# A hybrid attention block on one core: longer distances between dependent steps in chunks two to four, the norm's table a quarter ahead, the last output weights behind the branches'

## The chip, the core and the metric

The kernel runs on 1 core of one Trainium2 chip. The metric is device time in microseconds (us) of one execution; the time of a kernel is the median of its runs. TensorE (PE in the profile, PEld its weight loads) multiplies, VectorE (DVE), ScalarE (ACT) and GpSimd (POOL) do the rest, and SyncE (SP) issues nearly all transfers, in one queue.

## What is computed

One layer over 2048 tokens of width 1024, in float32, with two mixers side by side:

```python
def hybrid_layer(x, w_in, conv_w, a_log, dt_bias, dn_norm_w, sinks, w_branch, w_out, ln_g, ln_b, cos, sin):
    h = jnp.einsum("bsd,dc->bsc", x, w_in)
    ...
    o_a = chunked_gated_delta_rule(q_a, k_a, v_a, g, beta)
    ...
    y_b = banded_sink_attention(q_b, k_b, v_b, sinks) * jax.nn.silu(sw_z)
    merged = (jax.nn.sigmoid(gate_a) * jnp.einsum("bsc,cd->bsd", y_a, w_branch[0])
              + jax.nn.sigmoid(gate_b) * jnp.einsum("bsc,cd->bsd", y_b, w_branch[1]))
    out = jnp.einsum("bsd,de->bse", merged, w_out)
    r = (DEEPNORM_ALPHA * x + out).astype(jnp.float32)
    ...
    y = (r - mu) * lax.rsqrt(var + LN_EPS) * ln_g.astype(jnp.float32) + ln_b.astype(jnp.float32)
```

Branch A is a gated delta rule with 4 heads of 128: inside a block a triangular inverse, from block to block a state S per head that each block reads and updates. Branch B is attention over a window of 128 tokens with 8 query heads of 64 and a learned sink in each softmax.

## The kernel before

**Tiling.** The sequence is cut into four chunks of 512 tokens (T), each of four blocks of 128 (NB). Every large product is done as three matmuls on a high and a low part (`prods`, L184 to L186), so that a piece of dense work is a run of 128x512 or 128x256 matmuls. The split weights are kept in DRAM after chunk one (`kw_...`) and loaded again in each later chunk, 512 KB a load, through four buffers `wb` (L160).

**The order of the work** on TensorE is the order in which the program issues it; a small planner, the class `Order`, works it out while the program is written. It has a clock `now` in nanoseconds. Dense pieces (`dense`) advance it by their cost: PE_R = 216 for a 512-column matmul. Between the bits of a dense piece, `run` issues every small task that has come due. A small task is a generator that yields (cost, distance): its next step is due that distance after this one, which is the time the other engines are given to get its operands ready. If a dense piece needs a task to be over, `finish(name)` jumps the clock from due time to due time and issues the steps without dense work between them:

```python
    def finish(self, name):
        while name not in self.done:
            self.run()
            if name not in self.done:
                self.now = min(t[0] for t in self.tasks)
```

The order of the dense pieces of a chunk stands in two strings, ORDER_FIRST for chunk one and ORDER for the others: `g` a gate, `kv`, `k0`, `q0`, `v0`, ... projections of branch A's heads and of the window, `w0` and `w1` the window's queries (`window_q`), `z` SiLU paths, `p` the output projection of the chunk before. A chunk's `kv`, `k0` and `q0` are issued early, between the branch pieces of the chunk before. VectorE, ScalarE and the queues get their order from the framework's scheduler, which goes by the order of the program and by what it takes to be ready.

**The small tasks.** The distances are the constants `LAT_...` in L40.
- `decays` (L299 on): the decay factors, with a step of 2000 between its sums and its transposes (L322).
- `front` of a head: transposes and products of q and k (L382, L395, L406, L426, L432), LAT_B apart. After L406 the blocks go to DRAM and back (L417, L419) to be inverted on VectorE (`inverse`, L947, L948); the result goes to DRAM (L445).
- `levels`: fetches the inverse (L458), waits LAT_D, and builds it up in four steps (L470, L477, L486, L491), LAT_B apart.
- `back`: the chain through the state. For each of four blocks L517 (reads S), L522 (reads `bt` of L519) and L528 (reads `wc` of L524, then L529 updates S), LAT_S apart: 12 steps a head.
- `query_rows`: transposes of the rotated queries (L584), LAT_Q after their projection. `window_q` itself calls `finish("qT0")` right behind the projection.
- `attend`: for each block of the window the scores (L610, L611), the softmax on VectorE and ScalarE (L618 to L630), LAT_SM later the transposes (L637), then the values (L645).
- `layer_norm` of the chunk before, on VectorE alone: four steps of statistics, then for each quarter of the width a table of 256 KB (L725, from `in_lnp`) and four steps with it (L727, L728).

`head_in` of head 3 calls `finish("back1")` ahead of k, and of head 2 `finish("vdone1")` ahead of v.

**The end.** In chunk four `branch_b` and `branch_a` (eight pieces each) load their weights `kw_b` as they go. Ahead of branch A's second and fifth piece `last_weights` loads a half of the first output weights (`kw_o`, 8 loads of 256 KB each time, L158) into buffers that x no longer needs; `last_project` uses them.

Of the kernel before, what the change touches and what calls it, by code (L numbers as in the profile page):

```python
# [8 lines left out]
F32 = mybir.dt.float32  # L9
# [30 lines left out]
LAT_INV, LAT_B, LAT_S, LAT_N, LAT_SM, LAT_D, LAT_M, LAT_K, LAT_Q, LAT_Y, LAT_F, LAT_W = 29600, 2700, 2300, 7700, 9200, 11000, 9000, 1400, 7900, 11500, 4100, 2300  # L40
# [4 lines left out]
ORDER = "kv k0 q0 v0 k1 p p p p q1 g w0 v1 z0 k2 q2 v2 g g g k3 z1 g q3 g w1 v3 g g g g z2 g g g z3 g g g"  # L45
# [18 lines left out]
def build(tc, xt, xn, wk, wg, par, lnp, cst, out, seq=2048):  # L64
    nc = tc.nc
    NCH = seq // T
    with ExitStack() as ctx:
# [196 lines left out]

        def window_kv(c):

            ww, more = [], ([w.rearrange("p (k c) -> p k c", k=2) for w in split(("kv", i), wk[i // 2, :, 528 * (i % 2):528 * (i % 2) + 528], 528)]
                            for i in range(4))
            ba = sm.tile([P, NB, 8], F32, name="ba")
            c.vs = [c.prev.vs[4] if c.i else None]  # L270
            for b0 in (0, 2):
                pss = [mm.tile([P, T], F32, name="mm")[:, :264] for _ in range(2)]
                yield from prod_tc(pss, (b0, b0 + 1), c.xh, c.xl, ww if b0 else kept(more, ww), lambda k: load_x(c, k))
                for b, ps in zip((b0, b0 + 1), pss):
                    if b >= 2:
# [8 lines left out]
            st.spawn("decay", decays(c, ba), LAT_Y)  # L284
# [14 lines left out]
        def decays(c, ba):  # L299
# [19 lines left out]
            yield 2 * 426, 2000  # L319
# [49 lines left out]
        def front(c, h):  # L369
# [22 lines left out]
            yield 4 * PE_T, LAT_B  # L392
# [10 lines left out]
            yield PE_R, LAT_B  # L403
# [7 lines left out]
            yield 4 * PE_F, LAT_B  # L411
# [17 lines left out]
            yield 4 * PE_T, LAT_B  # L429
# [6 lines left out]
            st.spawn(f"levels{h}", levels(c, h, m2, q_), max(LAT_B, t0 + LAT_INV - st.now))  # L436
            st.spawn(f"back{h}", back(c, h, k4, q_, ktl, qd, dt, cc, ksum, qsum), max(LAT_B, t0 + LAT_INV - st.now))
            yield 4 * PE_F, 0

        def inverse(h, su, xi):  # L440

            with tc.issue_after(next(i for i in reversed(nc.cur_bb.bb.instructions) if i.engine == mybir.EngineType.DVE)):
                nc.vector.memset(view(su, 33, [[66, 16]]), 0.0)
            yield from small_inverse(tc, pt.tile([P, 256], F32, name="xt"), su, xi.rearrange("p (c i) -> p c i", i=32))
            nc.sync.dma_start(out=at(scr_p[h % 2], 0, [[P, P], [1, P]]), in_=xi)  # L445
            yield None, 0

        def levels(c, h, m2, q_):
# [11 lines left out]
            yield 0, LAT_D  # L460
# [12 lines left out]
            yield 8 * PE_Q, LAT_B  # L473
# [9 lines left out]
            yield 12 * PE_Q, LAT_B  # L483
# [4 lines left out]
            yield 4 * PE_T, LAT_B  # L488
# [4 lines left out]
            yield 4 * PE_T, LAT_B  # L493

        def back(c, h, k4, q_, ktl, qd, dt, cc, ksum, qsum):
# [17 lines left out]
            yield 4 * PE_T, LAT_B  # L513
            psO = p4()
            for b in range(NB):
# [4 lines left out]
                yield PE_F, LAT_S  # L520
# [5 lines left out]
                yield 2 * PE_F, LAT_S  # L526
# [4 lines left out]
                yield 2 * PE_F, LAT_S  # L531
# [29 lines left out]
        def window_q(c, gp):  # L561

            if gp:
                st.finish("window0")
            c.qT = [pa.tile([P, NB, 2, P], F32R, name=n, bufs=1) for n in ("qT0", "qT1")]
            pss = [mm.tile([P, 2, 256], F32, name="mm") for _ in range(2)]
            yield from prod_all(pss, c.xh, c.xl, quarters([f"q{gp}{i}" for i in range(2)]), lambda k: load_x(c, k))
            for b0 in (0, 2):
                if b0:
                    st.finish("qT0")  # L570
                qr = [pa.tile([P, 256], F32, name="kr") for _ in range(2)]
                for b in range(2):
                    rope(nc, sm, qr[b], pss[b0 // 2][:, b], 4, cos[:, c.i * NB + b0 + b], sin[:, c.i * NB + b0 + b])
                st.spawn(f"qT{b0}", query_rows(c, b0, qr), LAT_Q)
# [19 lines left out]
        def attend(c, gp):  # L594
# [8 lines left out]
            for b in range(NB):  # L603
# [27 lines left out]
                yield 8 * PE_T, LAT_SM  # L631
# [80 lines left out]
        def layer_norm(c):  # L712
            fs = []
            for b in range(NB):
# [6 lines left out]
                yield None, 2500  # L721
            for eg in range(4):
                es = slice(256 * eg, 256 * eg + 256)
                lg = pa.tile([P, 2, 256], F32, name="s")
                nc.sync.dma_start(out=lg, in_=bass.AP(tensor=lnp.tensor, offset=lnp.offset + 256 * eg, ap=[[0, P], [D, 2], [1, 256]]))  # L725
                for r, rs, mu in fs:
                    nc.vector.scalar_tensor_tensor(r[:, es], r[:, es], mu, lg[:, 0], ALU.subtract, ALU.mult)  # L727
                    nc.vector.scalar_tensor_tensor(r[:, es], r[:, es], rs, lg[:, 1], ALU.mult, ALU.add)  # L728
                    yield None, 1800
# [70 lines left out]
        for i in range(NCH):  # L800
# [24 lines left out]
            for d in range(KT):  # L825
                if i == NCH - 1 and d in (1, 4):
                    last_weights(c, d // 3)
                st.dense([branch_a(c, d)])
# [195 lines left out]
```

## Time and profile before

| | us |
|---|---|
| median of 3 runs (lowest, highest) | 1668.41 (1666.62, 1669.23) |
| the profiled execution | 1672.24 |
| its span, first to last instruction | 1670.4 |
| TensorE busy in it | 1618.9 |
| VectorE, ScalarE, GpSimd busy | 969.3, 596.2, 92.9 |

Mean granted TensorE clock in the profiled execution: 0.986 of full. The end of a matmul in the profile is modelled, since matmuls are pipelined: from start to start is what one costs, and idle time is counted from the modelled end of the one before. A row of waits names the engine, the tile that it writes and the line, then what came last among the things it waited for: us in total, times, longest. Chunk one ends at about 412 us, two at 830, three at 1240; chunk four's gates end at 1570, and the last projection begins at about 1615.

### The profile page before, as it was taken

To read this page: it belongs to the slowest core of one execution; us is meant where nothing else is said; L and a number is where in the kernel's file an instruction comes from. 1 tells how busy PE (TensorE), PEld (TensorE's weight loads), DVE (VectorE), ACT (ScalarE), POOL (GpSimd) and SP (SyncE) were. 2 spreads that over 40 slices of the span, in tenths; PEclk is the share of its full clock that TensorE was granted. 3 is DMA by queue.
4 is the path that set the end of the run, shared out by engine and by line. 5 is a ranking of instruction groups with operands and counts; after the bars stand their busy time and mean duration, and the time that the engine had idled before them with its cause. 6 is when DMAs were issued, how large, how long until landed. Compare 5 with 4: busy or idle time off the path is not lost.

```text
span 1670.4 us, 26939 instructions
## 1 busy us (share of the span) xinstructions
PE 1618.9 (97%) x9846; PEld 1368.2 (82%) x9846; DVE 969.3 (58%) x3005; ACT 596.2 (36%) x1688; POOL 92.9 (6%) x142
## 2 busy tenths in 40 slices
PE   8999999999998999999999999999999999999998
PEld 6877878787987878788898878888889887878788
DVE  5777687459566656323747774623482866462145
ACT  3565455424213533441301452433230254233110
POOL 2100000000000001000000000000000100000000
PEclk9999999999999999999999999999999999999999
DMA  8876575776867446457666644646666654555862
GB/s 310 260 232 222 184 245 190 244 235 216 273 207 213 135 130 168 142 163 237 191 213 205 199 128 145 172 137 190 202 190 210 221 162 119 166 162 145 284 214 83
DMA packets 189157, 323.37 MB, mean 194 GB/s; under 512 B 31072, under 2 KB 45408, under 8 KB 188896
## 3 DMA queue, kind: packets, MB, share of 16 engines
q1 hardware_dynamic: 185184, 316.40, 60.6%
q0 software_dynamic: 3840, 5.25, 1.5%
q8 instruction: 78, 1.28, 0.3%
q14 instruction: 55, 0.45, 0.1%
HBM read 244.97 MB, written 71.37 MB: 189 GB/s over the span
## 4 chain that ended last, share of the span: by engine, by line
PE 82%; DVE 7%; DMA 7%; ACT 2%; issue 1%; SPq 1%; POOL 0%; DVEq 0%; ACTq 0%; POOLq 0%
PE mm L184 22%; PE mm L186 22%; PE mm L185 22%; PE pp L645 2%; PE pp L637 2%; DMA s<-in_lnp 2%; DMA w<-in_xt 1%; PE pp L610 1%; PE pp L611 1%; PE pd L432 1%; DVE wb L165 1%; PE pd L517 1%; PE pd L528 1%; DMA xl<-kw_o 1%; PE pd L406 1%
## 5 line engine op out<-in xcount | busy, mean ns | idle before, releaser
L184 PE MATMUL mm<-xh,wb 128*128 128x512 f32 x1128 | 468.6, 415 | 0.0
L186 PE MATMUL mm<-xh,wb 128*128 128x512 f32 x1128 | 448.0, 397 | 0.0
L185 PE MATMUL mm<-xl,wb 128*128 128x512 f32 x1128 | 446.8, 396 | 0.0
L186 PEld LDWEIGHTS mm<-xh,wb 128*128 128x128 f32 x1128 | 213.7, 189 | 50.3
L184 PEld LDWEIGHTS mm<-xh,wb 128*128 128x128 f32 x1128 | 214.5, 190 | 45.6 <-issue 6.5
L185 PEld LDWEIGHTS mm<-xl,wb 128*128 128x128 f32 x1128 | 215.2, 191 | 38.8
L184 PE MATMUL mm<-wb,xh 128*128 128x256 f32 (+1 forms) x384 | 113.5, 296 | 1.8 <-DVE kr L899 0.9
L184 PE MATMUL mm<-wb,s 128*128 128x256 f32 x384 | 110.4, 287 | 0.0
L185 PE MATMUL mm<-wb,xh 128*128 128x256 f32 (+1 forms) x384 | 108.9, 284 | 0.0
L186 PE MATMUL mm<-wb,xl 128*128 128x256 f32 (+1 forms) x384 | 108.7, 283 | 0.0
L185 PE MATMUL mm<-wb,s 128*128 128x256 f32 x384 | 108.4, 282 | 0.0
L186 PE MATMUL mm<-wb,s 128*128 128x256 f32 x384 | 108.4, 282 | 0.0
L165 DVE TENSOR_TENSOR wb<-w,wb 128x512 fp32r<-128x512 f32 (+1 forms) x110 | 75.4, 686 | 46.3 <-ACT wb L164 45.5
L164 ACT ACTIVATE wb<-w 128x512 fp32r<-128x512 f32 (+1 forms) x110 | 69.1, 629 | 84.4 <-PE mm L186 58.1
L623 ACT ACTIVATE s<-s,nm 128x256 f32<-128x256 f32 (+1 forms) x128 | 62.5, 490 | 57.1 <-DVE nm L620 56.6
L947 DVE TENSOR_TENSOR xt<-su,xi 128x16 f32<-128x16 f32 (+15 forms) x256 | 76.3, 298 | 5.3
L948 DVE TENSOR_REDUCE xi<-xt 128x8 f32<-128x16 f32 (+15 forms) x256 | 74.6, 291 | 4.9
L184 PEld LDWEIGHTS mm<-wb,xh 128*128 128x128 f32 x384 | 72.9, 190 | 2.7 <-issue 2.5
L184 PEld LDWEIGHTS mm<-wb,s 128*128 128x128 f32 x384 | 73.1, 190 | 0.8
L185 PEld LDWEIGHTS mm<-wb,xh 128*128 128x128 f32 x384 | 72.9, 190 | 0.5
L185 PEld LDWEIGHTS mm<-wb,s 128*128 128x128 f32 x384 | 73.0, 190 | 0.1
L186 PEld LDWEIGHTS mm<-wb,s 128*128 128x128 f32 x384 | 73.0, 190 | 0.0
(660 smaller groups left out, 2997.4 us busy)
## 6 DMA issues: line engine op xcount, KB each, us to landing
wb<-kw_h SPq DMA_DIRECT2D x96, 512.0 KB, 4.1
wb<-kw_g SPq DMA_DIRECT2D x96, 512.0 KB, 4.0
w<-in_wg SPq DMA_DIRECT2D x106, 256.0 KB, 4.2
wb<-kw_b SPq DMA_DIRECT2D x48, 512.0 KB, 4.4
wb<-kw_o SPq DMA_DIRECT2D x36, 512.0 KB, 4.1
kw_h<-wb SPq DMA_DIRECT2D x32, 512.0 KB, 3.9
kw_g<-wb SPq DMA_DIRECT2D x32, 512.0 KB, 3.7
wb<-kw_q SPq DMA_DIRECT2D x24, 512.0 KB, 3.9
```

The source lines that it names most:

```text
L164: nc.scalar.activation(hi, raw, AF.Copy)
L165: nc.vector.tensor_tensor(lo, raw, hi.bitcast(F32), ALU.subtract)
L184: nc.tensor.matmul(ps, sh, mh, start=(first and i == 0), stop=False, skip_group_check=shared)
L185: nc.tensor.matmul(ps, sh, ml, start=False, stop=False, skip_group_check=shared)
L186: nc.tensor.matmul(ps, sl, mh, start=False, stop=(last and i == n), skip_group_check=shared)
L406: nc.tensor.matmul(psKK[:, b], k4[:, b], k4[:, b], start=True, stop=True)
L432: nc.tensor.matmul(psKQ[:, b], k4[:, b], q4[:, b], start=True, stop=True)
L623: nc.scalar.activation(ss[v][:, g, k0:], ss[v][:, g, k0:], AF.Exp, bias=nm[:, v, g:g + 1], scale=0.125, accum_out=su[:, v, g:g + 1])
L637: nc.tensor.transpose(psp[:, kb, g], ss[v][:, g, P * kb:P * kb + P], ident)
L645: nc.tensor.matmul(psY[64 * v:64 * v + 64], c.vs[b + kb][:, 64 * v:64 * v + 64], pTs[v][:, kb], start=(kb == kbs[0]), stop=(kb == 1))
L947: nc.vector.tensor_tensor(tx[:, :, :, :n], u, x, ALU.mult)
L948: nc.vector.tensor_reduce(xi[:, :, i:i + 2], tx[:, :, :, :n], AX.X, ALU.add)
```

## The change

The distances become pairs, the first for chunk one and the second for the others; chunk one's are as before. One gate moves from ahead of `w1` to behind it. The norm's steps are spaced wider, and its table for a quarter is fetched one quarter ahead. `last_weights` is issued with an edge to the latest SP instruction, so that its loads come behind it in the queue.

```diff
-LAT_INV, LAT_B, LAT_S, LAT_N, LAT_SM, LAT_D, LAT_M, LAT_K, LAT_Q, LAT_Y, LAT_F, LAT_W = 29600, 2700, 2300, 7700, 9200, 11000, 9000, 1400, 7900, 11500, 4100, 2300
+LAT_INV, LAT_N, LAT_M, LAT_K, LAT_F, LAT_W = 29600, 7700, 9000, 1400, 4100, 2300
+
+LAT_B, LAT_S, LAT_SM, LAT_D, LAT_Q, LAT_Y, LAT_G = (2700, 3300), (2300, 2900), (9200, 11500), (11000, 13000), (7900, 10500), (11500, 11500), (2000, 3500)
...
-ORDER = "kv k0 q0 v0 k1 p p p p q1 g w0 v1 z0 k2 q2 v2 g g g k3 z1 g q3 g w1 v3 g g g g z2 g g g z3 g g g"
+ORDER = "kv k0 q0 v0 k1 p p p p q1 g w0 v1 z0 k2 q2 v2 g g g k3 z1 g q3 w1 g v3 g g g g z2 g g g z3 g g g"
...
+        latest = lambda engine: next(i for i in reversed(nc.cur_bb.bb.instructions) if i.engine == engine)
...
-            yield 2 * 426, 2000
+            yield 2 * 426, LAT_G[c.i > 0]
...
-            yield 4 * PE_T, LAT_B
+            yield 4 * PE_T, LAT_B[c.i > 0]
...
         def layer_norm(c):
-            fs = []
+            fs, lgs = [], []
+
+            def load_lg(eg):
+                lgs.append(pa.tile([P, 2, 256], F32, name="s"))
+                nc.sync.dma_start(out=lgs[eg], in_=bass.AP(tensor=lnp.tensor, offset=lnp.offset + 256 * eg, ap=[[0, P], [D, 2], [1, 256]]))
+
+            load_lg(0)
...
-                yield None, 2500
+                yield None, 2600
             for eg in range(4):
                 es = slice(256 * eg, 256 * eg + 256)
-                lg = pa.tile([P, 2, 256], F32, name="s")
-                nc.sync.dma_start(out=lg, in_=bass.AP(tensor=lnp.tensor, offset=lnp.offset + 256 * eg, ap=[[0, P], [D, 2], [1, 256]]))
+                if eg < 3:
+                    load_lg(eg + 1)
+                lg = lgs[eg]
                 for r, rs, mu in fs:
...
-                    yield None, 1800
+                    yield None, 2200
...
                 if i == NCH - 1 and d in (1, 4):
-                    last_weights(c, d // 3)
+                    with tc.issue_after(latest(mybir.EngineType.SP)):
+                        last_weights(c, d // 3)
                 st.dense([branch_a(c, d)])
```

The other uses of LAT_B, LAT_S, LAT_SM, LAT_D, LAT_Q and LAT_Y take `[c.i > 0]` in the same way.

## Rows read from the trace of the kernel before

**Rows 1.** The page, busy time of each engine.
```profile
PE 1618.9 (97%) x9846; PEld 1368.2 (82%) x9846; DVE 969.3 (58%) x3005; ACT 596.2 (36%) x1688; POOL 92.9 (6%) x142
```
**Rows 2.** Who waited for whom, TensorE, whole span: total us, times, longest.
```profile
PE pp L637 <- ACT s L630: 6.4, 3, 2.1
...
PE mm L184 <- DMA wb<-kw_b: 2.6, 2, 1.6
```
**Rows 3.** The same list for chunk two, 412 to 830 us.
```profile
PE pp L584 <- DVE rsq L884: 3.4, 1, 3.4
...
PE pd L470 <- DMA p__4808<-scrp: 1.9, 1, 1.9
PE pd L528 <- DVE wc L524: 1.1, 3, 0.6
PE pp L584 <- DVE rr L886: 0.8, 1, 0.8
PE pd L522 <- DVE bt L519: 0.7, 2, 0.4
PE pd L517 <- DVE S L529: 0.6, 1, 0.6
```
**Rows 4.** The same list for chunk three, 830 to 1240 us.
```profile
PE pd L517 <- DVE S L529: 1.8, 2, 1.6
PE pd L395 <- DVE ktl L385: 1.1, 1, 1.1
```
**Rows 5.** The same list for chunk four, 1240 to 1560 us.
```profile
PE pd L517 <- DVE S L529: 2.5, 1, 2.5
...
PE pd L395 <- DVE ktl L385: 1.2, 1, 1.2
```
**Rows 6.** Busy time by stretch: PE, PEld, DVE, ACT, POOL, granted clock, DMA share, GB/s.
```profile
440.31:443.73 3.42, 3.42 (x28) 3.36 (x23) 1.48 (x5) 0.27 (x1) 0.00 (x0) 0.50 0.96 302
508.58:515.41 6.83, 5.87 (x16) 4.46 (x17) 6.52 (x38) 2.33 (x5) 1.08 (x2) 0.50 0.98 360
```
**Rows 7.** Timeline of TensorE: start us, duration us, line, operation, tiles.
```profile
518.87 0.39 PE L186 MATMUL mm<-xh,wb 128*128 128x512 f32 x1
519.10 0.39 PE L184 MATMUL mm<-xh,wb 128*128 128x512 f32 x1
```
**Rows 8.** Transfers: kw_b over the span, over 1565 to 1590 us; a stretch of these.
```profile
wb<-kw_b SPq DMA_DIRECT2D x48, 512.0 KB, 4.4
...
wb<-kw_b SPq DMA_DIRECT2D x8, 512.0 KB, 7.3
...
1575.00:1580.00 5.00, 5.00 (x23) 4.06 (x22) 1.38 (x2) 0.00 (x0) 0.00 (x0) 1.00 1.05 387
```
**Rows 9.** Timeline of VectorE in chunk three's norm.
```profile
909.27 0.88 DVE L727 SCALAR_TENSOR_TENSOR yBh<-yBh,mv,s 128x256 f32<-128x256 f32 x2 [1.45 <-DMA s<-in_lnp]
910.07 0.88 DVE L727 SCALAR_TENSOR_TENSOR yBl<-yBl,mv,s 128x256 f32<-128x256 f32 x2
```
**Rows 10.** Timeline of VectorE ahead of chunk two's query transposes.
```profile
507.17 0.67 DVE L433 TENSOR_TENSOR dt<-pd,dt 128x512 f32<-128x512 f32 x1 [1.93 <-issue]
```
**Rows 11.** Timeline of TensorE in chunk two's finish of back1.
```profile
587.19 0.28 PE L611 MATMUL pp<-kTl,qT 128*128 128x256 f32 x1
...
589.54 0.49 PE L522 MATMUL pd<-bt,q__5694 128*128 128x128 f32 x2 [0.44 <-DVE bt L519]
...
590.47 0.49 PE L528 MATMUL pd<-wc,ktl 128*128 128x128 f32 x2 [0.22 <-DVE wc L524]
...
593.32 1.15 PE L637 MATMUL pp<-ct,s 128*128 128x128 f32 x4 [2.13 <-ACT s L630]
```
**Rows 12.** Head 2's inverse in chunk four: timeline of TensorE, and the loads of L458.
```profile
1380.83 1.06 PE L406 MATMUL pd<-k 128*128 128x128 f32 x8
...
L458 SPq DMA_DIRECT2D p__14897<-scrp x4: 309/424/429, 1414.6 to 1415.9; - x4
...
DMA to landing us min/median/max: 1.6/1.7/1.8
...
1425.78 0.21 PE L470 MATMUL pd<-p__14897,m 32*32 32x32 f32 x1
```

More of the change, by code (lines that the diff above doesn't have):

```diff
@@ L283, in window_kv @@
                     st.spawn(f"kT{b}", key_rows(c, b, kr), LAT_K)
-            st.spawn("decay", decays(c, ba), LAT_Y)
+            st.spawn("decay", decays(c, ba), LAT_Y[c.i > 0])
         def key_rows(c, b, kr):
@@ L402, in front @@
             nc.vector.tensor_tensor(qd, qd, q4, ALU.mult)
-            yield PE_R, LAT_B
+            yield PE_R, LAT_B[c.i > 0]
             psKK = p4()
@@ L410, in front @@
             t0 = st.now
-            yield 4 * PE_F, LAT_B
+            yield 4 * PE_F, LAT_B[c.i > 0]
             sm_ = scr_m[h % 2]
@@ L428, in front @@
                 nc.scalar.activation(junk, psQ[:, b], AF.Square, accum_out=qsum[:, b:b + 1])
-            yield 4 * PE_T, LAT_B
+            yield 4 * PE_T, LAT_B[c.i > 0]
             psKQ = p4()
@@ L435, in front @@
             q_ = t4("q_", 2)
-            st.spawn(f"levels{h}", levels(c, h, m2, q_), max(LAT_B, t0 + LAT_INV - st.now))
-            st.spawn(f"back{h}", back(c, h, k4, q_, ktl, qd, dt, cc, ksum, qsum), max(LAT_B, t0 + LAT_INV - st.now))
+            st.spawn(f"levels{h}", levels(c, h, m2, q_), max(LAT_B[c.i > 0], t0 + LAT_INV - st.now))
+            st.spawn(f"back{h}", back(c, h, k4, q_, ktl, qd, dt, cc, ksum, qsum), max(LAT_B[c.i > 0], t0 + LAT_INV - st.now))
             yield 4 * PE_F, 0
         def inverse(h, su, xi):
-            with tc.issue_after(next(i for i in reversed(nc.cur_bb.bb.instructions) if i.engine == mybir.EngineType.DVE)):
+            with tc.issue_after(latest(mybir.EngineType.DVE)):
                 nc.vector.memset(view(su, 33, [[66, 16]]), 0.0)
@@ L459, in levels @@
                                   in_=at(scr_p[h % 2], 1024 * i, [[32, 32], [4096, NB], [1, 32]]))
-            yield 0, LAT_D
+            yield 0, LAT_D[c.i > 0]
             for i in range(4):
@@ L472, in levels @@
                 copy[s](x_[hi[s], :, :32], ps[s][hi[s], :, :32])
-            yield 8 * PE_Q, LAT_B
+            yield 8 * PE_Q, LAT_B[c.i > 0]
             ps = [p4(), pp.tile([P, NB, P], F32, name="pp")]
@@ L482, in levels @@
                 copy[1 - s](q_[lo[s], :, hi[s]], ps[s][lo[s], :, :32])
-            yield 12 * PE_Q, LAT_B
+            yield 12 * PE_Q, LAT_B[c.i > 0]
             ps = p4()
@@ L487, in levels @@
             copy[0](x_[64:], ps[64:, :, :64])
-            yield 4 * PE_T, LAT_B
+            yield 4 * PE_T, LAT_B[c.i > 0]
             ps = p4()
@@ L492, in levels @@
             copy[1](q_[:64, :, 64:], ps[:64, :, :64])
-            yield 4 * PE_T, LAT_B
+            yield 4 * PE_T, LAT_B[c.i > 0]
         def back(c, h, k4, q_, ktl, qd, dt, cc, ksum, qsum):
@@ L512, in back @@
             st.done.add(f"vdone{h}")
-            yield 4 * PE_T, LAT_B
+            yield 4 * PE_T, LAT_B[c.i > 0]
             psO = p4()
@@ L519, in back @@
                 nc.vector.scalar_tensor_tensor(bt, ps, c.neG[:, b, h:h + 1], vt[:, b], ALU.mult, ALU.add)
-                yield PE_F, LAT_S
+                yield PE_F, LAT_S[c.i > 0]
                 ps = pd.tile([P, T], F32, name="pd")[:, :P]
@@ L525, in back @@
                 nc.tensor.matmul(psO[:, b], qd[:, b], S[:, h], start=True, stop=False)
-                yield 2 * PE_F, LAT_S
+                yield 2 * PE_F, LAT_S[c.i > 0]
                 ps = pd.tile([P, T], F32, name="pd")[:, :P]
@@ L530, in back @@
                 nc.tensor.matmul(psO[:, b], dt[:, b], wc, start=False, stop=True)
-                yield 2 * PE_F, LAT_S
+                yield 2 * PE_F, LAT_S[c.i > 0]
             osum = sm.tile([P, NB], F32, name="osum")
@@ L573, in window_q @@
                     rope(nc, sm, qr[b], pss[b0 // 2][:, b], 4, cos[:, c.i * NB + b0 + b], sin[:, c.i * NB + b0 + b])
-                st.spawn(f"qT{b0}", query_rows(c, b0, qr), LAT_Q)
+                st.spawn(f"qT{b0}", query_rows(c, b0, qr), LAT_Q[c.i > 0])
             for g in range(2):
@@ L630, in attend @@
                     nc.scalar.activation(ss[v][:, g, k0:], ss[v][:, g, k0:], AF.Copy, scale=su[:, v, g:g + 1])
-                yield 8 * PE_T, LAT_SM
+                yield 8 * PE_T, LAT_SM[c.i > 0]
                 pTs = []
```

## The prediction

> **What bounds the kernel now.** The page comes first: TensorE is busy 1618.9 of 1670.4 us [rows 1], in an order fixed by hand, so every wait in that order adds to the time and nothing else does. The list of who waited for whom comes second, for TensorE alone: two entries that lie wholly behind chunk one are the first transpose of a softmax block, 2.13 us late once in each of chunks two to four, and a branch weight, 1.6 and 1.0 us late near the end [rows 2]. The same list by chunk holds the rest: chunk two [rows 3], chunk three [rows 4], chunk four [rows 5]. With the softmax that is 10.6 + 5.0 + 5.8 us in the three chunks and 2.6 at the end, 24 in all; what else the lists hold is under 0.9 us each. Third, the granted clock: six stretches in these chunks at 0.50 of full clock, the lower of its two levels (1.2 GHz), five of 3.41 us as the first shown and one of 6.83 [rows 6]. Each begins at a stall of 1.9 to 3.4 us, while stalls of 1.6 us elsewhere [rows 2, 4] were followed by none. A drop of 3.41 us costs up to half of it, 1.7 us; the long one, in which the engine was busy for 5.87 us, 2.9. Together 5 x 1.7 + 2.9 = 11.4. So about 35 us (2.1%) is all that better distances could return.
>
> **The change part by part.** Distances work through dense matmuls: a step due 600 ns later on the planner's clock has 600 ns more of dense work before it. The planner counts 216 ns for a 512-column matmul, the trace shows 230 from start to start [rows 7], so 0.6 us on paper is 0.65 on the engine. But where the planner meets a finish() that isn't done, it jumps its clock and issues steps with no dense work between. There a longer distance buys nothing, and only makes the jump longer. I walked the planner's clock from the code's costs, old and new. Jumps per chunk, old: 8.3 (qT0 of w0), 1.9 (vdone1), 8.3 (back1), 8.8 (qT0 of w1). New: 10.9, 6.5, 14.7, 10.9 in chunk two and 10.9, 5.5, 19.1, 10.9 in three and four. The third is the one that grows: head 1's chain starts 2.0 + 4 x 0.6 = 4.4 later and runs 0.6 + 12 x 0.6 = 7.8 longer, the earlier jump gives back 3.6, and rounding up to whole dense pieces (1.3 each) makes the rest of +10.8.
>
> *Last output weights.* 16 loads of 256 KB stand among the branch loads on SP's queue, whose median landing there is 7.3 us [rows 8]. Behind branch A's first and fourth load they no longer delay branch B: -2.6; bounds 0 and -2.6. A branch piece is 12 matmuls of 0.23 us [rows 7], 2.8 us, so the last projection wants them 7 and 4 pieces later, 19 and 11 us; the wait comes back if branch A's loads now land late (rivals).
>
> *Head 0's inverse in chunk two* (L470, 1.9 us late [rows 3], and one drop): the distance grows by 2.0, which the walk makes 2.6 of dense work, 2.8 real, more than 1.9. -1.9 - 1.7 = -3.6; bounds 0 and -3.6.
>
> *Back and front steps in chunk two* (L517, L522, L528: 2.4 us [rows 3]) gain 0.65 each, but later ones slide into the first jump: -1.2. *L395 in three and four* (1.1 and 1.2 [rows 4, 5]): 0.65 each, -1.3; bounds 0 and -2.3.
>
> *The norm's table.* VectorE stood 1.45 us for the table, and a burst of the norm's steps followed [rows 9]; TensorE then waited 1.6 us in chunk three and 2.5 in chunk four for L529, a state update on the same engine [rows 4, 5], the latter with a drop. Fetched a quarter (4 x 2.2 us) ahead, the table is there: -1.6 - 2.5 - 1.7 = -5.8; bounds 0 and -5.8. The 12 loads only move ahead on SP's queue by one quarter; the two buffers they rotate through are free by then, and the weights beside them have four. Spacing 1.8 to 2.2 costs VectorE nothing: softmax waits for the norm's end either way, and the walk has window0 start at the same dense work in both.
>
> *Query transposes in chunk two* (L584: 3.4 + 0.8 us, drop 2.9 [rows 3, 6]): qT0 is a forced finish, so its 10500 gives no cover. VectorE itself stood 1.93 us there with nothing shown to wait for [rows 10]. Other steps come between now, which may or may not remove it: bounds 0 and -7.1; I take a third, -2.5, since the row that delayed it isn't touched.
>
> *The price of the jumps.* In w0's jump of chunks three and four two chain steps stand without dense work where one did, with the norm running: +0.5 each, +1.0. In back1's jump the step before the softmax, L610, falls inside the jump too. Its softmax took from 587.5 to 593.3, 5.8 us, with a chain step every 0.93 us beside it [rows 11]. Old: a jump from 588.6 (one step before L522) to the transposes' end at 593.8, 5.2 us with 1.2 of matmuls in it, 4.0 lost. New, in three and four: L645 1.0, one further us until its PSUM buffer is read (an estimate from the 0.93 of a chain step), L610 0.9, softmax 5.8, transposes 0.9, so 9.6 with 4.1 of matmuls: 5.5 lost, +1.5 each; in chunk two +0.9. The idle piece in it becomes about 3.6 us, as long as the one that had the long drop [rows 3, 6]: +1.0 for each of three. Sum +6.9; bounds +0 (the softmax alone counts) and +12.
>
> *Head 2's inverse.* Its L470 came 44.9 us after L406, and its operand landed 1.8 us after the last of the loads that were issued from 1414.6 to 1415.9, some 37 us after L406: 8 us of slack [rows 12]. The walk leaves 16.8 of dense work there in chunks three and four where 25.9 was, 9.8 us real, given back in part by the longer jump (2 to 3): between no wait and 2 us with a drop. +0.7.
>
> *w1 before a gate, LAT_G, LAT_SM and LAT_Q elsewhere, window_q's 12 weight loads ahead of a gate's 2 on SP, and the qT copies on POOL's queue ahead by as much*: the rows show no wait there, and finish(window0) is met without a jump: 0; if that cover goes, w1's softmax pays what window0's does.
>
> Sum: -2.6 - 3.6 - 1.2 - 1.3 - 5.8 - 2.5 + 1.0 + 6.9 + 0.7 = **-8.4 us**. The profiled execution took 1672.24 us, 3.8 over the median of 1668.41, so 1663.8 against its own time and **1660.0** against the median.
>
> **The rivals.** *Slower: the jumps decide.* A chain step in a jump costs 0.2 to 0.45 us where VectorE is free [rows 11], but 1.6 where it had a backlog [rows 4]. The walk has five such steps a chunk (two in w0, three in w1), 15 in all. At 1.6 instead of 0.35 each they add 18.8: 1678.8. The sum turns at 0.35 + 8.4/15 = 0.9 us a step. For it: the norm and head 1's inverse share VectorE with w0's jump. Against: the steps of today's back1 jump, with head 2's inverse beside them, show 0.2 to 0.45.
> *No change: two cures fail.* If the query stall stays whole (+2.5) and the L517 waits only move into w0's jump (+2.9, half of 5.8), -3.0 is left: 1665.4. For it: neither stall's row names a distance.
> *Branch A waits in branch B's place.* All these loads go through one queue and land in the order of issue, 387 GB/s at its fullest [rows 8]; eight loads (2.1 MB) ahead are 5.4 us, and the three buffers ahead of the one in use hide 3 x 2.8 = 8.4 us less the landing, 4.4 over the whole span [rows 8]. Then 1.4 us twice, and the 2.6 is lost: 1662.6. The Trainium skill's page "DMA: Bandwidth & Descriptors" (Queues, rings and completion order) says that each DMA engine consumes descriptors in ring order, which is this rule; by it a load moved back on SP delays whatever follows. The landing of 7.3 us behind the output weights agrees.
> *More: jumps are free.* If L637 is late by no more than today, the query stall goes whole and head 2 doesn't wait, -8.4 - 6.9 - 4.6 - 0.7 = -20.6: 1647.8.
> *The change doesn't do what it says* is part of the first two: distances without dense work are no distances.
>
> **How the numbers follow.** The forecast 0.37, branch A 0.07, more 0.14, no change 0.18, slower 0.24. A difference under 0.2% (3.3 us) can't be told from none. So faster 0.58, same 0.18, slower 0.24. The range goes from just under the case "more" to just under "slower", 1646 to 1677; the forecast's own is 1652 to 1665, from the bounds of the inverse and the norm's table at one end and of the query stall at the other.
>
> **What would show it.** Right: no kw_b wait near the end; no in_lnp wait on VectorE; no L470 wait in chunk two; L637 still late, by 3 us or more, in each chunk, with a drop; L522 or L528 waits at w0. Wrong: waits over 1 us on several steps of one jump (slower), L470 of head 2 late with a drop, or L637 gone from the list (more).

## The result, and the profile after

The changed kernel takes **1682.55 us** (median of 4 runs, 1681.66 to 1684.13), the one before 1668.82 beside it: ratio **1.0077 [1.0061, 1.0093]**, 13.7 us slower where 8.4 faster was forecast, and outside the range of 1646 to 1677. The profiled execution took 1682.04 us with a span of 1680.3, against 1672.24 and 1670.4.

The page's busy line answers to [rows 1]:

```profile
PE 1618.3 (96%) x9846; PEld 1367.9 (81%) x9846; DVE 974.7 (58%) x3005; ACT 596.1 (35%) x1688; POOL 94.5 (6%) x142
```

TensorE is busy as long as before. The time in which it is not went from 51.5 us (1670.4 - 1618.9) to 62.0, and that is the whole difference of the spans. (The spans differ by 9.9 us and the medians by 13.7. In the first 410 us, where only a few early steps of chunk two are changed, the profiled execution of before held 17.1 us at half clock and the changed one 6.8; that is worth up to 5 us.) So the question is which waits came, and the list of who waited for whom says it. Lines have moved by two to four: L517, L522 and L528 of the back steps are now L521, L526 and L532, L637 is L641, L529 is L533, L584 is L588; the norm's L727 and L728 are L738 and L739. First chunk two (408 to 830 us, [rows 3]):

```profile
PE pd L526 <- DVE bt L523: 4.7, 4, 2.0
PE pd L521 <- DVE S L533: 2.2, 2, 1.5
PE pd L532 <- DVE su L447: 1.3, 1, 1.3
PE pp L641 <- ACT s L634: 1.1, 1, 1.1
...
PE pp L474 <- DMA p__4839<-scrp: 0.5, 1, 0.5
```

Chunk three (830 to 1245, [rows 4]), and the first three of chunk four (1245 to 1570, [rows 5]):

```profile
PE pd L521 <- DVE S L533: 4.3, 2, 2.8
PE pd L526 <- DVE bt L523: 2.0, 2, 1.4
PE pp L641 <- ACT s L634: 2.0, 1, 2.0
...
PE pd L521 <- DVE S L533: 4.0, 2, 2.4
PE pd L526 <- DVE bt L523: 3.1, 3, 1.4
PE pp L641 <- ACT s L634: 2.0, 1, 2.0
```

What was to be cured is gone or small: the query transposes' own waits (3.4 and 0.8), the inverse's 1.9 (now 0.5), L395. What grew are the steps of one chain, each of which needs the VectorE result of the step before: L521 and L526 with 20.3 us in the three chunks, where L517 and L522 had 6.8.

**Where they stand**, for the most part, is in TensorE's timeline. The finish of qT0 in w0, chunk three, then the finish of back1:

```profile
911.50 0.49 PE L521 MATMUL pd<-S,k 128*128 128x128 f32 x2 [2.76 <-DVE S L533]
913.41 0.80 PE L526 MATMUL pd<-bt,q__8826 128*128 128x128 f32 x2 [1.42 <-DVE bt L523]
...
995.36 0.38 PE L532 MATMUL pd<-wc,ktl 128*128 128x128 f32 x2
...
997.54 0.49 PE L521 MATMUL pd<-S,k 128*128 128x128 f32 x2 [1.57 <-DVE S L533]
998.59 0.49 PE L526 MATMUL pd<-bt,q__9812 128*128 128x128 f32 x2 [0.56 <-DVE bt L523]
...
1001.27 1.30 PE L641 MATMUL pp<-ct,s 128*128 128x128 f32 x4 [1.97 <-ACT s L634]
```

From 992.8 to 1003.9 no dense matmul runs. In chunk two the finish of qT0 holds such waits too, 4.6 us with the two that follow these:

```profile
496.45 0.46 PE L526 MATMUL pd<-bt,q__4577 128*128 128x128 f32 x2 [2.04 <-DVE bt L523]
...
499.32 0.49 PE L532 MATMUL pd<-wc,ktl 128*128 128x128 f32 x2 [1.30 <-DVE su L447]
```

Before, the waits there were 4.9 us (0.65 for L528 and the query transposes' 3.44 and 0.76), with a long drop behind them. So the query transposes' waits were replaced, and what went is the drop. The granted clock follows (columns as in [rows 6]; chunk two's back1, then w0 and back1 of chunk three; chunk four repeats these two at 1329.0 and 1417.7):

```profile
584.80:591.63 6.83, 6.25 (x19) 4.99 (x20) 1.55 (x9) 3.61 (x12) 1.01 (x1) 0.50 0.11 20
912.50:919.33 6.83, 5.91 (x20) 5.03 (x21) 5.87 (x28) 2.02 (x5) 0.61 (x2) 0.50 0.74 295
1001.30:1004.71 3.41, 3.41 (x14) 3.10 (x15) 0.35 (x1) 2.90 (x11) 0.00 (x0) 0.50 0.17 33
```

Five stretches at the lower level, 27.3 us, where there were six with 23.9: the drops at the inverse and at the query transposes went, and longer ones came at w0 and at chunk two's back1.

**The norm's table** came no earlier. VectorE's waits for it, over the span, after:

```profile
DVE yBh L738 <- DMA s<-in_lnp: 14.1, 8, 2.8
```

It was 9.5 us in 6 waits. VectorE's and SP's timelines in chunk three:

```profile
900.29 0.15 DVE L898 SCALAR_TENSOR_TENSOR rs<-rsq,rs 128x1 f32<-128x1 f32 x1
900.48 0.88 DVE L739 SCALAR_TENSOR_TENSOR yBl<-yBl,rs,s 128x256 f32<-128x256 f32 x2
...
905.22 0.88 DVE L738 SCALAR_TENSOR_TENSOR yBh<-yBh,mv,s 128x256 f32<-128x256 f32 x2 [2.82 <-DMA s<-in_lnp]
...
910.24 0.88 DVE L739 SCALAR_TENSOR_TENSOR yBh<-yBh,rs,s 128x256 f32<-128x256 f32 x2
...
911.10 0.34 DVE L533 SCALAR_TENSOR_TENSOR S<-S,eGl,pd 128x128 f32<-128x128 f32 x1
...
900.99 0.89 SPq L721 DMA_DIRECT2D s<-in_lnp  x2
```

The third quarter's load is issued at 900.99, right behind the first of the two L739 that began at 900.48 and took 0.48 (VectorE starts them 0.40 apart): it waits for its buffer. The last block's factor rs was ready only at 900.3, and until its L739 has read the first quarter's table that buffer isn't free. VectorE stood 2.82 us, worked off the second half of the norm in one burst, and did the state update (L533) at 911.10, though its matmul had run at 906.5. That is the 2.76 us above. The kernel before did the same, with the same load behind the same reader:

```profile
905.05 0.87 DVE L728 SCALAR_TENSOR_TENSOR yBl<-yBl,rs,s 128x256 f32<-128x256 f32 x2
...
905.55 0.89 SPq L725 DMA_DIRECT2D s<-in_lnp  x2
```

**The last weights**: the wait for kw_b moved from branch B [rows 2] to branch A, as two rows of TensorE's timeline show by their operand:

```profile
1606.49 0.47 PE L186 MATMUL mm<-yAh,wb 128*128 128x512 f32 x1 [1.83 <-DMA wb<-kw_b]
1615.96 0.47 PE L186 MATMUL mm<-yAh,wb 128*128 128x512 f32 x1 [0.88 <-DMA wb<-kw_b]
```

2.7 us in all, as much as the 2.6 of before.

### The profile page after: what moved, and what is told of

Its sections match the earlier page's. It is cut to its first block, busy times and chain, and to the rows that moved or that the text cites. A ratio compares the mean times of both kernels' runs of the same rounds, so it can differ in the third digit from the quotient of the medians.

```text
span 1680.3 us, 26921 instructions
## 1 busy us (share of the span) xinstructions
PE 1618.3 (96%) x9846; PEld 1367.9 (81%) x9846; DVE 974.7 (58%) x3005; ACT 596.1 (35%) x1688; POOL 94.5 (6%) x142
## 3 DMA queue, kind: packets, MB, share of 16 engines
q8 instruction: 78, 1.28, 0.3%
## 4 chain that ended last, share of the span: by engine, by line
PE 79%; DVE 10%; DMA 7%; ACT 2%; issue 1%; SPq 1%; POOL 0%; DVEq 0%; ACTq 0%; POOLq 0%
PE mm L186 21%; PE mm L188 21%; PE mm L187 21%; PE pp L649 2%; PE pp L641 2%; DMA s<-in_lnp 2%; PE pp L614 1%; PE pd L532 1%; DMA w<-in_wg 1%; DVE wb L167 1%; DMA w<-in_xt 1%; DVE xi L960 1%; PE pp L615 1%; PE pd L526 1%; PE pd L534 1%
## 5 line engine op out<-in xcount | busy, mean ns | idle before, releaser
L186 PEld LDWEIGHTS mm<-wb,s 128*128 128x128 f32 x384 | 72.4, 189 | 1.8 <-DVE yBh L705 1.1
L188 PEld LDWEIGHTS mm<-wb,xl 128*128 128x128 f32 x384 | 72.4, 189 | 0.0
L187 PEld LDWEIGHTS mm<-wb,s 128*128 128x128 f32 x384 | 72.2, 188 | 0.1
```

What stands on the lines that cost most here:

```text
L186: nc.tensor.matmul(ps, sh, mh, start=(first and i == 0), stop=False, skip_group_check=shared)
L187: nc.tensor.matmul(ps, sh, ml, start=False, stop=False, skip_group_check=shared)
L188: nc.tensor.matmul(ps, sl, mh, start=False, stop=(last and i == n), skip_group_check=shared)
```

## The experiments

A step that a finish issues with no dense work since the step before it is called bare below; "the walk" is the walk of the planner's clock. Ratios are to the kernel before, run beside each.

### The parts alone

Each is the kernel before with one part: all distances (e1), the norm (e2), the last weights (e3), w1 one gate earlier (e4).

```
e1: LAT_B, LAT_S, LAT_SM, LAT_D, LAT_Q, LAT_Y, LAT_G as pairs, every use by [c.i > 0]
e2: + load_lg(eg + 1) a quarter ahead;  2500 -> 2600, 1800 -> 2200
e3: + with tc.issue_after(latest(mybir.EngineType.SP)): last_weights(c, d // 3)
e4: - q3 g w1 v3   + q3 w1 g v3
```

> Only the distances of the change; order, norm and last weights as before. Theory J (the longer jumps of finish() are what costs): 1679 to 1686, 10 to 17 us over before, with L517 and L522 late by over 1 us in w0's jump of chunks three and four. Rival N (the norm's new loads and spacing cost it, by holding VectorE): within 4 us of before. Rival M (parts add up badly, none alone costs much): 1670 to 1675.

> Only the norm's part: table a quarter ahead, spacing 2600 and 2200. Theory J: within 4 us of before, since the jumps stay 8.3, 1.9, 8.3, 8.8; and the table's third quarter is still waited for by VectorE (1 to 3 us a chunk), because its load stands in SP's queue behind weight loads that wait for a buffer. Rival N: 6 us or more over before. A third reading (the prefetch works, the gain was eaten elsewhere): 3 to 6 us under before and no in_lnp wait over 0.5 us.

> Only the output weights behind the branches'. Theory R (the loads go through one ring, so the wait moves from branch B to branch A): within 2 us of before, kw_b waits of 2 to 3 us in all, now at yAh. Rival (the wait goes): 2.6 us under before, no kw_b wait.

> Only w1 one gate earlier. Theory J: within 3 us of before; the planner's jumps stay 8.3 to 8.8, w1's holds one chain step more. Rival (w1's place is what costs): 4 us or more over before.

| run | median us | ratio [95%] |
|---|---|---|
| e1 | 1688.29 | 1.0092 [1.0076, 1.0108] |
| e2 | 1671.99 | 0.9997 [0.9981, 1.0012] |
| e3 | 1670.34 | 0.9993 [0.9979, 1.0006] |
| e4 | 1669.43 | 0.9990 [0.9977, 1.0004] |

The distances alone cost 15.4 us (0.92% of 1671.72, the median beside them), which is theory J's 10 to 17, and w0's jump in chunk three has its two waits (2.22 us at L521, 1.43 at L526). The other three can't be told from no change, and two of them carried 8.4 us of the forecast.

### Which jump, and what it costs

e5 loads the norm's table on POOL's queue, e6 shortens qT0's own distance, e7 moves one head projection out of the way of back1's finish, all in the changed kernel; e8 does the last two, with v2 and w1 moved too, in the kernel before.

```diff
e5 -nc.sync.dma_start(out=lgs[eg], ...
e5 +nc.gpsimd.dma_start(out=lgs[eg], ...
e6 -query_rows(c, b0, qr), LAT_Q[c.i > 0])
e6 +query_rows(c, b0, qr), 2000 if c.i and not b0 else LAT_Q[c.i > 0])
e7 -v2 g g g k3 z1 g q3 w1 g v3
e7 +v2 g g g z1 g k3 q3 w1 g v3
e8 +g v2 g g z1 g k3 q3 w1 g v3   and the 2000 of e6
```

> The changed kernel with the norm's table alone moved from SP's queue to POOL's, so that it no longer lands behind the weights issued before it. Theory A (the late table makes w0's jump dear: VectorE stood 2.8 us for it at 905.2 and then did the norm in one burst until 911.0, with the state update of L533 behind it): VectorE's waits for in_lnp fall from 14.1 us to under 4, TensorE's 2.8 us and 2.4 us waits for L533 in w0's jump shrink below 1 us and the drop of the clock behind them goes; time falls from 1682.6 to 1670-1676. Theory B (the steps without dense work cost by themselves, each by its way through VectorE and back, whatever the norm does): in_lnp waits go as well, but the waits for L533 and L523 in w0's jump stay within 1 us of 4.2 us, and the time stays within 1679-1683.

> The changed kernel with qT0's own distance set to 2000 in chunks two to four. By the walk of the planner's clock the jumps of w0 and w1 fall from 10.9 to 2.7 and 2.4, but the one of vdone1 grows from 5.5 to 16.5, and back1's goes from 19.1 to 13.9: 14 steps a chunk still stand without dense work (15 in the changed kernel, 5 to 6 in the one before). Theory A (what counts is the number of bare steps, some 0.7 us each): the time stays within 1678-1684, the waits for L533 and L526 in w0 go, and as much comes up at L477 to L491 and L395 to L410 in front of v1's end. Theory B (only bare steps beside the norm cost; elsewhere 0.2 to 0.45 us as in the kernel before): w0's 4.2 us and its drop go in chunks three and four and little comes back, 1670-1676. Rival C (2000 is too short for the rope on VectorE): waits of 2 us or more at L588 in both windows, slower than 1684.

> The changed kernel with k3 moved behind z1 and the gate after it, in chunks two to four. By the walk back1's jump falls from 19.1 to 4.9 (14.7 to 3.6 in chunk two) and its bare steps from 7 to 1; w0's stay 8. Theory A (each bare step costs some 0.7 us): the waits at L641, L614, L521 and L526 around back1 shrink, 6 fewer steps in three chunks are worth 8 to 13 us, 1670-1675. Theory B (the jump of back1 costs little more than the softmax that it waits for, 2 us a chunk, and that stays): under 3 us gained, 1679-1682. Theory C (the rest of the loss is w0's): the waits in w0, 4.2 and 3.9 us, do not change in either case.

> The kernel before, with its old distances, its norm and its last weights, but with qT0's own distance 2000 in chunks two to four and the order ... q2 g v2 g g z1 g k3 q3 w1 g v3 there: jumps of 2.4, 2.9, 3.3 and 2.4 by the walk instead of 8.3, 1.9, 8.3 and 8.8, and one bare step a chunk instead of 5 to 6. Theory A (bare steps are what costs): 4 to 5 fewer in each of three chunks, at 0.7 us some 9 us less, 1658-1664, with the waits at L637 and L517 gone or under 1 us. Theory B (a softmax or a query block that is needed waits for its data whether the planner jumps or not): waits of the same size come up at L584 and L610, and the time stays within 1667-1674. Rival C: the 2000 leaves the rope too little time, L584 waits 2 us or more twice a chunk with a drop each, 1676-1690.

| run | median us | ratio [95%] |
|---|---|---|
| e5 | 1683.72 | 1.0088 [1.0069, 1.0108] |
| e6 | 1712.59 | 1.0264 [1.0241, 1.0286] |
| e7 | 1663.29 | 0.9961 [0.9944, 0.9979] |
| e8 | 1658.50 | 0.9936 [0.9917, 0.9956] |

**e7** decides: one word of the order gives 19.3 us back, more than the change lost and more than theory A's 8 to 13. Its chunk three has no L641 any more, and L521 and L526 stand in w0 alone (1.1 us of the former 2.0, one wait of the former two):

```profile
PE pd L521 <- DVE S L533: 2.5, 1, 2.5
PE pp L614 <- ACT qT L594: 1.2, 2, 0.7
PE pd L526 <- DVE bt L523: 1.1, 1, 1.1
PE pd L430 <- DVE m L413: 0.8, 1, 0.8
```

**e5** didn't do what it was for. VectorE still waited 2.41 us, since the load (POOL's timeline, second row) starts behind the same L739, only from another queue. So the queue is not what holds the table; the buffer is.

```profile
909.11 0.88 DVE L738 SCALAR_TENSOR_TENSOR yBh<-yBh,mv,s 128x256 f32<-128x256 f32 x2 [2.41 <-DMA s<-in_lnp]
...
904.43 1.47 POOL L721 DMA_DIRECT2D s<-in_lnp  x2 [3.52 <-DVE yBl L739]
```

**e6** went as rival C said in time and in the first window, and further: the rope isn't ready in 2 us beside the norm (L588 is 2.3 to 4.7 us late there, 1.1 in the second window), and the rest of the chain slides into vdone1's jump, where L481 is 4.7 us late in each chunk. The number of bare steps (14 against 15 a chunk, by the walk) said nothing about its time.

```profile
PE pp L588 <- DVE kr L911: 15.7, 8, 4.6
...
PE pd L481 <- DVE q__5701 L467: 4.7, 1, 4.7
```

**e8** shows these edits paying in the kernel before, 0.64%; e9 says how much of it is back1's.

### Back1's jump before the change, and the distances taken back

```diff
e9  (before)  -v2 g g g k3 z1 g q3 g w1 v3
e9            +v2 g g g z1 g k3 q3 g w1 v3
e10 (e7)      LAT_B, LAT_S, LAT_Q back to 2700, 2300, 7900
e11 (before)  the order of e8, and 5000 for qT0 instead of 2000
e12 (changed) LAT_B, LAT_S back to 2700, 2300
```

> The kernel before with k3 alone moved behind z1 and the gate after it in chunks two to four: by the walk back1's jump (8.3) goes altogether, w0's and w1's stay. It prices the jump of back1 as it was before the change; the same edit in the changed kernel gave 19.3 us. Theory A (a jump costs by its length and by the steps in it, so the change made this one dearer): the wait at L637 (2.1 us) and the drop behind it go in each chunk, 8 to 12 us in all, 1658-1663, and the difference to 19.3 is what the change added here. Theory B (the jump of back1 cost the same before and after, and the change lost its time elsewhere): 17 to 20 us, 1650-1654. Theory C (the softmax is waited for at its next place anyway): under 3 us, 1667-1672.

> The changed kernel with k3 late (1663.3 so) and with the three distances back that lengthen w0's jump: LAT_S, LAT_B and LAT_Q as before. By the walk the jumps are 8.3, 3.4, none, 8.3 and the bare steps 5 a chunk instead of 9; the longer LAT_D, LAT_SM, LAT_G, the norm, w1's place and the last weights stay as changed. Theory A (in w0's jump the three distances only add bare steps): the waits for L533 and L523 in w0 fall from 3.6 to 4.0 us a chunk to some 1.8 us and the long drop goes, 1653-1659. Theory B (the three distances pay elsewhere, at L395 and L517 to L528): L399 waits 1.1 us again in chunks three and four, and what w0 gives back is lost, 1661-1666.

> The kernel before with the order of e8 (v2 and k3 later, w1 a gate earlier) and qT0's own distance 5000 instead of 2000 (7900 before): jumps 5.4, none, 3.3, 5.9, three to four bare steps a chunk instead of one. e8 ran at 1658.5 with waits of 1.0 to 1.4 us and of 0.5 us at L584, where the rope wasn't ready. Theory A (L584's waits were the price of the 2000): they go, but the bare steps' waits (L517, L522, L528) come up by 1 to 2 us a chunk; within 2 us of e8. Theory B (only the removed jump of back1 paid): the same time as e9, and L584 stays late by what its VectorE work takes.

> The changed kernel with LAT_S and LAT_B back at 2300 and 2700, everything else as changed, k3 at its place: by the walk the jumps are 10.9, none, 11.0, 11.4, and 12 to 13 bare steps a chunk stand instead of 15; back1's jump is 11.0 instead of 19.1 (14.7) with 6 instead of 7 bare steps. Theory A (the longer chain steps are what made back1's jump dear): 9 to 14 us of the 19 come back, 1669-1674. Theory B (the number of bare steps counts, not the length of the jump): 2 to 3 fewer a chunk at 0.7 us, 4 to 6 us, 1676-1679. Theory C (the softmax's own distance, 9200 to 11500, is what made it dear): under 3 us, 1680-1683.

| run | median us | ratio [95%] |
|---|---|---|
| e9 | 1658.12 | 0.9932 [0.9912, 0.9952] |
| e10 | 1657.56 | 0.9926 [0.9906, 0.9945] |
| e11 | 1667.64 | 0.9985 [0.9973, 0.9997] |
| e12 | 1665.94 | 0.9976 [0.9960, 0.9991] |

**e9**: back1's jump was worth 11.1 us already before the change. The same edit gives 19.3 in the changed kernel, so the change made it dearer by 8.2. That is theory A of e9. Most of the 11.1 is not waits but clock. In e9's profiled execution TensorE is idle for 49.9 us (1654.0 - 1604.1), only 1.6 less than before, since other waits came for the 6.4 us at L637; but chunks two to four have one stretch at half clock, 3.41 us, where there were 23.9 us, and 20.5 us less at half clock are worth up to 10.2 (the page's busy line of e9, and that stretch):

```profile
PE 1604.1 (97%) x9846; PEld 1358.8 (82%) x9846; DVE 973.9 (59%) x3005; ACT 596.7 (36%) x1688; POOL 92.5 (6%) x142
...
508.30:511.71 3.41, 3.41 (x10) 2.62 (x9) 3.20 (x19) 1.51 (x4) 1.09 (x2) 0.50 1.02 382
```

**e12**: with LAT_S and LAT_B old, 16.6 us come back, more than theory A's 9 to 14, and what is left of the change is a little faster than the kernel before. L641 is gone from chunk three's list, though k3 stands where it stood:

```profile
PE pd L526 <- DVE bt L523: 2.4, 3, 1.0
PE pd L521 <- DVE S L533: 2.0, 2, 1.8
PE pd L532 <- DVE wc L528: 1.1, 2, 0.8
PE pp L614 <- ACT qT L594: 1.0, 1, 1.0
```

**e10** against e7 (5.7 us, theory A): with back1's jump out of the way the three distances still cost, in w0, where chunk three's waits for L533 and L523 went from 2.52 and 1.11 us to 1.28 and 0.71, and the stretch at half clock from 6.83 to 3.41 us; a wait of 1.07 for L523 came 7 us ahead of them. The intervals of the two ratios just touch. Against e9 (0.6 less): all the rest of the change together bought nothing that can be told. **e11** was a miss of both theories, 9 us slower than e8: L477 waits 1.7 us in each chunk with it, and a drop stands beside.

### One distance each, and the inverse alone

```diff
e13 (changed) LAT_S back to 2300
e14 (changed) LAT_B back to 2700
e15 (e9)      -yield 0, LAT_D
e15           +yield 0, 13000 if c.i else LAT_D
```

> The changed kernel with LAT_S alone back at 2300 (LAT_B stays 3300). Both old together gave 1665.9 where the changed kernel takes 1682.6. By the walk back1's jump falls from 19.1 (14.7) to 9.4 with 4 bare steps instead of 7, while w0's stays at 10.9 with 8 to 9 and vdone1's at 6.5. Theory A (the length of back1's jump is what costs: its end is set by four back steps, one of LAT_B and three kinds of LAT_S in series): nearly all of the 16.6 us comes back, 1665-1669. Theory B (the number of bare steps counts): 2 to 3 fewer a chunk, 1676-1679. Theory C (LAT_B's steps cost as much as LAT_S's): about half, 1673-1676.

> The changed kernel with LAT_B alone back at 2700 (LAT_S stays 2900): by the walk vdone1's jump goes (5.5 before), back1's stays long, 17.6 instead of 19.1 (14.7 in chunk two), with the same 7 bare steps. Theory A (the length of back1's jump): almost nothing comes back, 1679-1684. Theory B (the sum of all jumps, 46.4 to 39.4 a chunk): 5 to 7 us, 1675-1678. Theory C (LAT_B's steps cost as much as LAT_S's): about half of 16.6, 1673-1676.

> The kernel before with k3 late (1658.1 so) and, of the change, LAT_D alone: 13000 in chunks two to four. It prices the one cure that worked for itself, L470 of head 0 in chunk two (2.3 us late with k3 late; I had put 3.6 us on it with the drop). By the walk a jump of 4.9 at vdone1 instead of 1.9, bare steps 3 to 5 as before. Theory A (the cure is worth its wait, with no drop behind it in the profile of that kernel): 1.5 to 2.5 us faster, 1655.5-1657. Theory B (the longer distance goes into vdone1's jump and the wait comes back there): within 1 us of 1658.1.

| run | median us | ratio [95%] |
|---|---|---|
| e13 | 1678.45 | 1.0044 [1.0026, 1.0063] |
| e14 | 1694.18 | 1.0138 [1.0115, 1.0162] |
| e15 | 1655.23 | 0.9903 [0.9879, 0.9927] |

e13's time lies in the range of theory B, the count of bare steps (1676 to 1679), but its rows don't show fewer waits of the chain: L521 and L526 wait 22.3 us in the three chunks, more than the changed kernel's 20.3, and what went is L641's 5.1. No theory held in e14. 4.1 us back for one distance, 11.6 lost for the other, 16.6 back for both: the distances don't add up. In e14 a new wait decides, head 2's inverse, 3.4 to 3.8 us late in each chunk. Chunk three's L474, the loads it reads, the landing of these:

```profile
1018.37 0.24 PE L474 MATMUL pd<-p__10740,m 32*32 32x32 f32 x2 [3.42 <-DMA p__10740<-scrp]
...
L462 SPq DMA_DIRECT2D p__10740<-scrp x4: 308/424/430, 1015.1 to 1016.4; - x4
...
DMA to landing us min/median/max: 2.5/3.0/3.3
```

So the length of back1's jump alone doesn't set the price; each distance shifts several chains against each other, and the latest of them pays. **e15** prices the inverse's cure: 2.9 us against e9 by the medians (4.8 by the ratios, whose intervals overlap), and it is the fastest kernel of the study, 16 us under the one before.

### The norm's backlog

The whole table is loaded once, at the norm's start, into yAh's buffer, which stands empty there: in the changed kernel (e16), in e15 (e17), in e7 (e18).

```diff
-lgs.append(pa.tile([P, 2, 256], F32, name="s"))
+lg = py.tile([P, 2, D], F32, name="yAh")
-... mu, lg[:, 0], ALU.subtract, ALU.mult)
+... mu, lg[:, 0, es], ALU.subtract, ALU.mult)
```

> The changed kernel with the norm's whole table (128x2048) loaded once, at the norm's start, into the buffer of yAh, which stands empty there, instead of quarter by quarter into two buffers. On POOL's queue the third quarter's load was still issued only at 904.4, right behind the L739 that freed its buffer, landed at 909.1 and was waited for 2.4 us; so it is the buffer, not the queue, that holds it. Theory A (the late third quarter pushes the norm's second half into w0's jump, and that is what the 2.8 us and 2.4 us waits for L533 there are): VectorE's in_lnp waits fall from 14.1 us to under 4, the waits for L533 and L523 in w0's jump fall by half or more, one long drop a chunk goes; 1671-1677. Theory B (bare steps wait whatever the norm does): the in_lnp waits go, and the time stays within 1680-1684.

> The fastest kernel so far (the one before with k3 late and LAT_D 13000, 1655.2) with the whole table in yAh's buffer. There w0's jump is 8.3 with 3 to 5 bare steps. Theory A: the waits at L528 and L517 in w0 (1.6 to 1.8 us) shrink and 2 to 5 us are gained, 1650-1653.5. Theory B: within 1.5 us of 1655.2.

> The changed kernel with k3 late (1663.3) and the whole table: both suspects of the changed kernel out of the way, its longer distances kept. It has still w0's jump of 10.9 with 8 bare steps. Theory A (norm's table is the other half of the loss): 1653-1657, as fast as the old distances with k3 late (1658.1) or faster. Theory B (w0's bare steps by themselves): within 2 us of 1663.3.

| run | median us | ratio [95%] |
|---|---|---|
| e16 | 1679.99 | 1.0060 [1.0041, 1.0079] |
| e17 | 1656.29 | 0.9914 [0.9892, 0.9935] |
| e18 | 1659.77 | 0.9936 [0.9919, 0.9953] |

VectorE has no in_lnp wait in any of the three, and the 2.8 us wait of w0 is gone: the same jump of e16's chunk three, with as many bare steps, has no drop and only these two waits:

```profile
913.95 0.49 PE L526 MATMUL pd<-bt,q__8820 128*128 128x128 f32 x2 [0.82 <-DVE bt L523]
...
914.88 0.49 PE L532 MATMUL pd<-wc,ktl 128*128 128x128 f32 x2 [0.22 <-DVE wc L528]
```

So the mechanism of theory A in e16 is shown. But the list of that chunk has a new wait in front, and L521's one wait is back1's:

```profile
PE pd L410 <- DVE bt L523: 2.1, 1, 2.1
PE pp L641 <- ACT s L634: 2.0, 1, 2.0
PE pd L521 <- DVE S L533: 1.6, 1, 1.6
PE pd L526 <- DVE bt L523: 1.4, 2, 0.8
```

L410 waits some 8 us ahead of w0's jump for a step of the back chain, which now stands behind the norm's instructions there. By the medians the table's lateness was worth 2.6 us (e16; 1674.3 to 1681.9) or 3.5 (e18), between the two theories, and in e17 nothing; the intervals of the ratios overlap with those of the kernels beside which they are set, so a gain in time isn't shown. The profiled run of e16 (1674.31) is its fastest, so its rows show less loss than its median.

## Why the prediction was wrong

Four differences of medians form a chain that sums to the change: before to e9 -11.1, e9 to e10 -0.6, e10 to e7 +5.7, e7 to the changed kernel +19.3, in all +13.3 against 13.7 measured. Sorted by the forecast's steps:

| step | forecast | runs |
|---|---|---|
| back1's jump | +6.9 | +8.2 (19.3 - 11.1) |
| LAT_S, LAT_B, LAT_Q elsewhere: w0's jump +1.0, back and front steps -1.2, L395 -1.3, query transposes -2.5 | -4.0 | +5.7 (e7 less e10) |
| head 0's inverse | -3.6 | -2.9 (e15 less e9) |
| table -5.8, last weights -2.6, head 2 +0.7, w1 and the others 0 | -7.7 | +2.3 (-0.6 + 2.9) |
| sum | -8.4 | +13.3 |

Medians move by 1 to 2 us from batch to batch, and e13 with e14 shows that parts don't add exactly, so the last column is an account, not four measurements. LAT_SM and LAT_G were not run alone; with back1's jump out of the way they stand, with the rest, in the 0.6 us between e9 and e10.

**Right**: that the time lies in waits in a fixed order and in the drops of the clock behind them; what the change adds to back1's jump (+6.9, by the runs +8.2), and how: the softmax falls inside the jump, which in chunk three has 4.1 us of waits and a 3.41 us drop where 5.5 lost and a drop were forecast. The inverse's cure fits as well. The price of the whole jump was too high (4.0 lost, where its own rows hold 2.8 of waits, and 1.7 of clock, times three, is 17; measured 11.1), and the sign given for it, L637 late by 3 us or more, didn't come: as L641 it was 1.1 to 2.0 late, since the chain steps ahead of it waited too. The query transposes' waits and drop went whole, not a third, but 4.6 us of chain waits, which had no term, came in the same jump. Head 2's slack was used up as walked: 1008.4 less 970.4 is 38.0 us from L410 to L474 in chunk three, where chunk four had 44.9 before [rows 12]; no wait came of it in the changed kernel, but in e14 the same place costs 3.4 to 3.8 us a chunk.

**Wrong, step one: "The two buffers they rotate through are free by then."** I looked at the queue and at the burst [rows 9], not at what releases the buffer. The first quarter's table is read by four blocks, the last of which has its factor only when VectorE has come through all four statistics; the load can't start earlier, however early it is written in the order. The row that would have told it was there: SP's issue of the third load beside the L739 that ends just before it. And even with the table there, at most 2.6 to 3.5 us came back by the medians, not 5.8, since the norm's work then meets the chain earlier (L410).

**Wrong, step two: w0's jump at +0.5 in chunks three and four.** I priced two more bare steps at the 0.2 to 0.45 us of a jump with a free VectorE [rows 11], although the norm runs beside this one. They took 2.76 and 1.42 us with 6.83 us at half clock, against 1.61 [rows 4]; in the two chunks together 8.0 us of waits and 13.7 us at half clock stand in this jump where 4.4 and 3.4 stood. Steps one and two hang together: with the table early the same jump waits 0.82 and 0.22 us (e16), so the price was near that of a free VectorE, and VectorE wasn't free. The rival "slower" had named the place (w0, VectorE's backlog) and its price of 1.6 us a step; it was given 0.24 and put its time at 1678.8, 3.8 under the result. Its count of 15 steps at one price was not right either: of the three a chunk that it put in w1 only one was over 1 us late, in chunk two (1.46 us), and e6, e12 and e14 missed what a count of bare steps alone would give.

**Wrong, step three: the last weights' -2.6.** The rival "branch A waits in branch B's place" came out as written, 2.7 us in two waits. The rule that it rested on, from the Trainium skill's page "DMA: Bandwidth & Descriptors" (Queues, rings and completion order), that each DMA engine consumes its descriptors in ring order, agrees with the trace: what is moved back on SP delays the loads that then stand behind it. That loads land in the order of issue is more than the rule says, for the Trainium skill's page adds that completion is not first in, first out; it is the trace of the kernel before that shows it, for every load that SP issued from 1557 to 1620 us.

**The sign** turned on the small gains. Six of them, 17.0 us together, were most of them taken near their full size, as if the step moved out of a stall found nothing at its new place. In the trace L521 and L526 grew by 13.5 us in the three chunks while the named stalls shrank.

## What to carry to other kernels

Where a scheduler forces something to finish, longer distances between dependent steps are spent inside that finish, with nothing to cover them: look for the finish and move what forces it (here one projection, 11 us before the change and 19 after it), before lengthening any distance. A prefetch is as early as the release of its buffer, so read which instruction is the buffer's last reader and when its own inputs are there. And price a step in a jump by the busiest state of the engine that it goes through, not by a quiet jump's.

## What was not expected of the hardware

The size of a stall alone doesn't tell whether the clock falls. In e17 three stalls of 2.26, 2.58 and 2.58 us (L406, one a chunk), with dense work on both sides, were followed by no stretch at 1.2 GHz, and none stands in that kernel between 400 and 1600 us; in the changed kernel stalls of 1.57, 0.56 and 1.97 us with some 4 us of small matmuls before and between them (the second timeline above) were. The row of e17's waits, 400 to 1600 us:

```profile
PE pd L406 <- DVE S L529: 7.4, 3, 2.6
```

Nor does the same stall end the same way each time. Near 380 us, at the end of chunk one, the transposes of the decays were late by the same 1.55 us before (first row) and after the change, and only in the execution of before did a stretch of 3.41 us at half clock follow, at 382.3:

```profile
381.10 0.60 PE L322 MATMUL pd<-ct,ghl 128*8 128x128 f32 x4 [1.55 <-DVE ghl L312]
...
378.31 0.60 PE L326 MATMUL pd<-ct,ghl 128*8 128x128 f32 x4 [1.55 <-DVE ghl L316]
```

So what the prediction read from its rows, that stalls of 1.9 us and more are followed by a drop and those of 1.6 are not, held in chunks two to four of the kernel before, and not in its chunk one or in e17. The Trainium skill's page "TensorE: Matmul & The Clock Gate" (A second HAM failure mode: psum-queue depth-cycling) tells of a kernel in which short idle pieces between groups of matmuls make the clock go back and forth. The stalls of 1.57, 0.56 and 1.97 us look like it; no run here shows the cause that it names.
